# Loading 32 conditioning tiles inside the S5 loop instead of ahead of it

## The chip, the cores and the metric

One core of a Trainium2 chip runs the kernel. The metric is device time in microseconds (us), the median of several executions. PE is TensorE, DVE is VectorE, ACT is ScalarE, POOL is GpSimd, and SP is the queue from which most loads are issued.

## The reference

One decoder layer on x of 1024 tokens by 1024 channels, all in f32, cut to what matters here:

```python
cond = silu(c)                                   # one vector of 1024
mod = cond @ ada_w + ada_b                       # 6 * 1024 values
sh1, sc1, gt1, sh2, sc2, gt2 = split(mod, 6)
h = rmsnorm(x, norm_mix_w) * (1 + sc1) + sh1     # first norm
q, f, i, g, u = split(h @ w_in)
mixed = concat([hgrn2(q, f, i, g), s5(u)]) @ w_out
x = x + gt1 * mixed                              # gate 1
h2 = rmsnorm(x, norm_ffn_w) * (1 + sc2) + sh2    # second norm
x = x + gt2 * peer(h2)                           # gate 2
out = rmsnorm(x, final_norm_w)
```

The hgrn2 part is a gated linear recurrence with 4 heads, s5 is a complex diagonal recurrence with 32 groups, and peer picks 16 of 16384 experts for each token and head.

## The kernel before

The product `cond @ ada_w` is not done on PE. `ada_w` lies in 48 tiles of 128 x 1024 (512 KB each), and for each tile DVE multiplies it with the broadcast `cond` and sums along the row (line 193), which gives one column of `mod`. Tiles 0 to 15 are scale and shift of the first norm and are needed at once; they go through a ring of 10 buffers called `ada`. Tiles 16 to 47 (gate 1, second norm, gate 2) are first needed after the S5 loop, in `out_proj`, `norm_T` of the second norm and `row_consts`. They go through the ring `row`, 5 buffers that they share with the tiles of x.

Ahead of the S5 loop stand `u_proj` (the S5 inputs, matmuls of line 328, weights loaded at line 323) and the first norms (line 288). `s5_setup` is a long row of tiny DVE instructions that makes the tables of powers. For each of 8 blocks of S5 groups `s5_tables` then lets POOL build `bsrc` (lines 493 to 495) and the cosine tables (521 to 523), DVE build `ca`, and PE transpose `bsrc` (line 528) and multiply (535). `s5_scan` (lines 554 to 579) runs one block, with DVE at 558 to 575. In the same loop `head_pieces` spreads the four HGRN heads: `hgrn_in` (four projections, line 328, and DVE at 683 to 700) and `hgrn_out` (DVE at 728 to 783, PE at 743).

No engine's order is written out by hand: a scheduler takes the instructions in program order and puts each into its engine's row by a timeline of its own. Every engine then runs its row strictly in that order, and so does the SP queue. The helper `issue_after(later, earlier)` is a hint to that scheduler about order; it adds no semaphore. `marks["base"]` is the list of projection matmuls made so far, two for each weight tile.

Of the kernel before, what the change touches and what calls it, by code (L numbers as in the profile page):

```python
# [10 lines left out]
F32 = mybir.dt.float32  # L11
# [11 lines left out]
P = 128  # L23
S = 1024
D = 1024
# [38 lines left out]
NROW = 5  # L64
# [27 lines left out]
def hymba_kernel(  # L92
# [22 lines left out]
    nc = tc.nc  # L115
# [3 lines left out]
    def T(pool, shape, dt, tag, bufs=None):  # L119
        return pool.tile(shape, dt, name=f"{tag}_{next(cnt)}", tag=tag, bufs=bufs)  # L120
# [13 lines left out]
    gp = ctx.enter_context(tc.tile_pool(name="gp", bufs=1, side="right"))  # L134
# [51 lines left out]

    mod = T(cst, [P, 48], F32, "mod")

    def ada(n0, n1, pool=None):
        for n in range(n0, n1):  # L190
            at = T(pool, [P, D], F32, "ada", bufs=10) if pool else T(gp, [P, D], F32, "row", bufs=NROW)
            nc.sync.dma_start(at, ada_t[n])
            nc.vector.tensor_tensor_reduce(
                out=at, in0=at, in1=cond["B"], scale=1.0, scalar=0.0, op0=ALU.mult, op1=ALU.add,
                accum_out=mod[:, n : n + 1],
            )
        TT(mod[:, n0:n1], mod[:, n0:n1], adab[:, n0:n1], ALU.add)
# [4 lines left out]
    def load_x(c, rows=False):  # L202
        t0, nt = CHUNKS[c]
        if rows:
            xt = [T(gp, [P, D], F32, "row", bufs=NROW) for _ in range(NBC)]
        else:
            xt = [T(tp, [P, D], F32, "xh", bufs=NBC) for _ in range(NBC)]
        for i, xi in enumerate(xt):
            nc.sync.dma_start(xi, x[t0 + i * P : t0 + (i + 1) * P, :])
        return xt  # L210
# [49 lines left out]
    def issue_after(later, earlier):  # L260
        tc.add_manual_dep(
            later.ins, earlier.ins.name, mybir.DependencyInfo(mybir.DependencyClass.NoSync, mybir.DependencyReason.DATA),
            reason="issue order",
        )

    marks = {"base": [], "pre": [], "dense": []}
    phase = ["base"]

    def diags_of(xt):
        rstd = rstd_of(tp, xt)  # L270
        diags = []
        for tb in range(NBC):
            dg = T(tp, [P, P], F32, "diag", bufs=4)
            TS(dg, ident, rstd[:, tb : tb + 1], None, ALU.mult)
            diags.append(dg)
        return diags
# [562 lines left out]
    for o, i, ni, j, nj in pieces_:  # L839
        n = max(ni, nj)  # L840
# [380 lines left out]
    with tc.tile_pool(name="ap", bufs=1) as ap_:  # L1221
        for k in range(0, KD, 2):
            ada(8 + k, 10 + k, ap_)
            STT(s1c[:, k : k + 2], mod[:, 8 + k : 10 + k], 1.0, nmw[:, k : k + 2], ALU.add, ALU.mult)
            ada(k, k + 2, ap_)
            if k == 0:
                x2 = load_x(NCK - 2, True)
                d2 = diags_of(x2)
            for c, xt, dg in ((3, x3, d3), (2, x2, d2)):
                hTs[c] += norm_T(xt, s1c, mod[:, 0:8], None, dg, (k,))  # L1230

    def head_pieces(c, two=False):

        t = {}
        outs = []
        far = T(gp, [P, 2, 2, TC], F32, "acc") if c == 2 else None

        def last(h):
            outs.append(hgrn_out(hp, c == NCK - 1, h, t.pop(h), two, None if far is None else far[:, h // 2]))
            if not two:  # L1240
                raws.setdefault(c, []).append((outs[-1][:, 0], outs[-1][:, 1]))

        for h in range(0, HEADS, 1 if two else 2):
            if len(t) == 2:
                last(min(t))
                yield
            t[h] = hgrn_in(hp, h, hTs[c], hTs[c + 1] if two else None)
            yield
        for h in sorted(t):
            last(h)  # L1250
            yield
        if two:
            for i in range(2):
                raws[c + i] = [(outs[h][:, i], outs[h + 1][:, i]) for h in range(0, HEADS, 2)]
# [16 lines left out]
    def step(what, c):  # L1271

        nonlocal rp
        if what == "n":
            hTs[c] = norm_T(*pre[c][:1], s1c, mod[:, 0:8], None, pre[c][1])
            heads[c] = head_pieces(c)
        elif what == "h":
            next(heads[c])
        elif what == "g":
            mixes[c] = s5_out(c)  # L1280
        elif what == "o":
            xts[c] = load_x(c, c == NCK - 1)
            hg = [r for two in raws[c] for r in two]
            out_proj(c, hg + mixes[c], xts[c])
        elif what == "N":
            h2Ts[c] = norm_T(xts[c], s2c, mod[:, 24:32], CHUNKS[c][0])
        elif what in "rR":
            routes[c] = score(c, h2Ts[c], h2Ts[c + 1] if what == "R" else None)
            next(routes[c])
        elif what == "s":  # L1290
            next(routes[c])
        elif what == "p":
            choose(rp, c)
        elif what == "X":
            next(heads[NCK - 1], None)
            hpx.close()
        elif what == "Y":
            rpx.close()
            rp = tb_["r"] = rp2x.enter_context(tc.tile_pool(name="rp2", bufs=1, side="right"))
        elif what == "Z":  # L1300
            tbx.close()

    hgrn_consts(hp)
    with tc.tile_pool(name="sp", bufs=1) as sp:
        prm = s5_setup(sp)
        tabs = [s5_tables(sp, b, prm, "hg") for b in range(2)]
        pieces = head_pieces(0, True)
        for b in range(NGB):
            s5_scan(sp, b, tabs[b])
            if b + 2 < NGB:  # L1310
                tabs.append(s5_tables(sp, b + 2, prm, "tr"))
            if b == N2B:
                step("n", 2)
            next(pieces, None)
            if b < 4:
                ada(16 + 8 * b, 24 + 8 * b)
            if b == PRB:
                for c in (2, 3):
                    pre[c] = load_x(c, True)
                    pre[c] = pre[c], diags_of(pre[c])  # L1320
        for _ in pieces:
            pass
# [120 lines left out]
```

## Time and profile before

| | |
|---|---|
| median of 3 runs | 3045.52 us (3045.49 to 3056.46) |
| the profiled execution | 3048.81 us, its span 3047.0 us |
| PE busy in the span | 2778.7 us (91%) |
| DVE busy in the span | 2520.5 us (83%) |
| mean granted PE clock | 0.964 of full speed |

The profiled execution is 3.3 us (0.1%) above the median of the runs, and 1.8 us of it lie outside the span. A row of the profile names the line, the engine and the tiles; times are from the start of the span.

### The profile page before, as it was taken

The page shows a single profiled execution, that of the slowest core. Times are in us where ns is not written, and L with a number is a line of the kernel's source. Part 1 is how long each engine was busy: PE and PEld are TensorE (multiplying, and loading weights), DVE is VectorE, ACT ScalarE, POOL GpSimd, SP SyncE. Part 2 cuts the span into 40 slices and gives each one's busy share as a digit, 9 for nine tenths or more (in the row PEclk, how much of TensorE's full clock was granted, in tenths as well). Part 3 has the DMA queues.
Part 4 walks back from the last instruction along what each step waited for, and adds up shares of the span by engine and source line. Part 5 has one row for each costly group of instructions (what it writes and reads, how often), then busy time and mean ns, then how long its engine had stood idle before and what let it go on. Part 6 is the DMA issues. An engine that isn't in the chain of part 4 may idle for free.

```text
span 3047.0 us, 45997 instructions
## 1 busy us (share of the span) xinstructions
PE 2778.7 (91%) x16071; PEld 2492.1 (82%) x16071; DVE 2520.5 (83%) x5862; ACT 1011.4 (33%) x2089; POOL 1132.2 (37%) x1043
## 2 busy tenths in 40 slices
PE   6898989989989999999879999999999999999970
PEld 5777879878878899999878888888888888888850
DVE  7868835987799999997867888887988887888987
ACT  4223432322211755654623222222222222222210
POOL 1754100031111013333334554544545454545645
PEclk9999999999999999999989999999999999999985
DMA  9722344486754469989999998999999898999967
GB/s 335 260 76 62 103 145 143 127 272 207 247 175 139 177 234 340 322 317 345 345 324 334 338 323 309 327 323 318 309 339 349 296 318 305 321 310 336 329 242 268
DMA packets 375112, 814.06 MB, mean 267 GB/s; under 512 B 60000, under 2 KB 153824, under 8 KB 369760
## 3 DMA queue, kind: packets, MB, share of 16 engines
q0 software_dynamic: 110592, 402.70, 37.6%
q1 hardware_dynamic: 226096, 386.12, 36.7%
q10 hardware_dynamic: 38192, 22.31, 2.6%
q8 instruction: 126, 2.06, 0.3%
q14 instruction: 106, 0.87, 0.1%
HBM read 730.96 MB, written 80.05 MB: 266 GB/s over the span
## 4 chain that ended last, share of the span: by engine, by line
PE 49%; DMA 17%; DVE 16%; issue 9%; POOL 6%; ACT 3%; ACTq 0%; SPq 0%; POOLq 0%; DVEq 0%
PE mm L1081 21%; PE mm L328 12%; DMA vraw<-in_v_rows_dram 5%; DMA row<-in_v_rows_dram,ei 4%; POOL row L947 4%; PE hg L1157 4%; PE tr L1157 3%; PE s L1157 3%; DVE acc L988 2%; DVE row L972 2%; DMA row<-in_u_rows_dram,ei 1%; PE s L1045 1%; PE hg L743 1%; PE s L1046 1%; DMA S<-sd 1%
## 5 line engine op out<-in xcount | busy, mean ns | idle before, releaser
L1081 PE MATMUL mm<-h2T,w 128*128 128x320 f32 x6144 | 950.6, 314 | 45.5 <-ACT S L1083 39.8
L1081 PEld LDWEIGHTS mm<-h2T,w 128*128 128x128 f32 x6144 | 920.1, 191 | 53.8 <-ACT S L1083 44.2
L947 POOL DMA_INDIRECT row<-in_u_rows_dram,ei x384 | 458.0, 1193 | 1247.4 <-DVE dots L972 700.3
L947 POOL DMA_INDIRECT row<-in_v_rows_dram,ei x384 | 511.9, 1333 | 474.4 <-DVE acc L988 389.2
L328 PE MATMUL mm<-hT,w 128*128 128x256 f32 x2304 | 530.7, 384 | 9.2 <-DMA w<-in_w_q_dram 3.8
L988 DVE SCALAR_TENSOR_TENSOR acc<-row,dots,acc 128x1024 f32<-128x1024 f32 x381 | 488.2, 1281 | 44.4 <-DMA row<-in_v_rows_dram,ei 41.3
L328 PEld LDWEIGHTS mm<-hT,w 128*128 128x128 f32 x2304 | 433.3, 193 | 66.7 <-issue 5.0
L972 DVE CUSTOM_DVE_ANT_0 row<-row,h2n 128x1024 f32<-128x1024 f32 x384 | 463.5, 1218 | 26.6 <-DMA row<-in_u_rows_dram,ei 26.6
L1157 PE MATMUL hg<-v,W 128*128 128x512 f32 x1296 | 356.4, 396 | 31.2 <-ACT v L257 19.4
L1157 PE MATMUL s<-v,W 128*128 128x512 f32 x1296 | 351.4, 393 | 2.8 <-DVE dacc L1170 2.0
L1157 PE MATMUL tr<-v,W 128*128 128x512 f32 x1248 | 339.0, 391 | 5.2 <-ACT v L257 2.8
L257 ACT CAST v<-vraw 128x512 fp32r<-128x512 f32 x256 | 158.8, 621 | 515.0 <-DMA vraw<-in_v_rows_dram 291.2
L1157 PEld LDWEIGHTS hg<-v,W 128*128 128x128 f32 x1296 | 245.5, 191 | 87.0 <-ACT v L257 21.3
L1157 PEld LDWEIGHTS s<-v,W 128*128 128x128 f32 x1296 | 244.6, 189 | 56.1 <-DVE dacc L1170 3.0
L1157 PEld LDWEIGHTS tr<-v,W 128*128 128x128 f32 x1248 | 234.3, 189 | 56.4 <-ACT v L257 3.6
L258 DVE TENSOR_TENSOR v<-vraw,v 128x512 fp32r<-128x512 f32 x256 | 175.8, 687 | 118.1 <-ACT v L257 114.9
L257 ACT CAST w<-raw 128x512 fp32r<-128x512 f32 x256 | 158.8, 620 | 214.9 <-PE mm L1081 179.5
L258 DVE TENSOR_TENSOR w<-raw,w 128x512 fp32r<-128x512 f32 x256 | 175.6, 687 | 54.3 <-ACT w L257 47.7
L1083 ACT ACTIVATE S<-mm 128x320 f32<-128x320 f32 x256 | 109.0, 437 | 243.8 <-PE mm L1081 198.0
L257 ACT CAST W<-S 128x640 fp32r<-128x640 f32 x128 | 93.4, 731 | 218.9 <-PE s L1157 58.1
L1100 DVE TENSOR_TENSOR S<-S,gt 128x640 f32<-128x640 f32 x128 | 104.2, 821 | 41.9 <-DMA S<-sd 36.2
L1048 ACT ACTIVATE Gs<-s 128x256 f32<-128x256 f32 x320 | 97.6, 389 | 43.6 <-PE s L1046 37.4
(375 smaller groups left out, 3200.7 us busy)
## 6 DMA issues: line engine op xcount, KB each, us to landing
raw<-in_u_t_dram SPq DMA_DIRECT2D x256, 256.0 KB
vraw<-in_v_rows_dram SPq DMA_DIRECT2D x256, 256.0 KB
gd<-Gs SPq DMA_DIRECT2D x40, 1024.0 KB
gt<-gd SPq DMA_DIRECT2D x32, 1280.0 KB
w<-in_w_in_dram SPq DMA_DIRECT2D x56, 512.0 KB
w<-in_w_q_dram SPq DMA_DIRECT2D x48, 512.0 KB
sd<-S SPq DMA_DIRECT2D x60, 320.0 KB
S<-sd SPq DMA_DIRECT2D x60, 320.0 KB
```

The source lines that it names most:

```text
L257: nc.scalar.copy(hi, src)
L258: return nc.vector.tensor_tensor(lo, src, hi.bitcast(F32), ALU.subtract)
L328: ins = nc.tensor.matmul(out, w[:, k * P : (k + 1) * P], rhs[k], start=(k == 0), stop=(k == nk - 1))
L743: nc.tensor.matmul(blk(pt, c), blk(lh, c), blk(rh, c), start=True, stop=True)
L947: g = nc.gpsimd.indirect_dma_start(out=t, out_offset=None, in_=table, in_offset=bass.IndirectOffsetOnAxis(ap=idx, axis=0))
L972: nc.vector.tensor_tensor_reduce(out=ut, in0=ut, in1=h2, scale=1.0, scalar=0.0, op0=ALU.mult, op1=ALU.add, accum_out=dots[:, j : j + 1],)
L988: STT(acc, vt, w[:, j : j + 1], acc, ALU.mult, ALU.add)
L1048: nc.scalar.mul(gq[c][:, :, o8 + o4 : o8 + o4 + 4], pg[:, :, c * NI : (c + 1) * NI].rearrange("p t i -> p i t"), 1.0 / GSC,)
L1081: nc.tensor.matmul(pt, wk[:, i, kc], h2T[k][:, j, cs_], start=(n == 0), stop=(n == 3 * KD - 1))
L1083: ACT(g[:, cs_], pt, AF.Gelu)
L1100: TT(gv, gv, gtile[0][:, :, e % IG, :], ALU.mult)
L1157: nc.tensor.matmul(pv[tb], ws[e][:, a, tb * P : (tb + 1) * P], v2[:, b, :], start=(e == s and n == 0), stop=(e == s + SLAB - 1 and n == 2),)
```

## The change

The loop body that handles tiles 16 to 47 moves from iterations 0 to 3 of the S5 loop to iterations 2 to 5. The tiles get a ring of their own in the pool of the loop, `ada` with 3 buffers, in place of the 5 of `row`. Each load is told to be issued after the projection matmul that is 20 marks (five weight tiles) back from the last one made so far in the program.

```diff
-    def ada(n0, n1, pool=None):
+    def ada(n0, n1, pool=None, after=None):
         for n in range(n0, n1):
-            at = T(pool, [P, D], F32, "ada", bufs=10) if pool else T(gp, [P, D], F32, "row", bufs=NROW)
-            nc.sync.dma_start(at, ada_t[n])
+            at = T(pool, [P, D], F32, "ada", bufs=10 if after is None else 3) if pool else T(gp, [P, D], F32, "row", bufs=NROW)
+            ld = nc.sync.dma_start(at, ada_t[n])
+            if after is not None:
+                issue_after(ld, after)
...
-            if b < 4:
-                ada(16 + 8 * b, 24 + 8 * b)
+            if b >= 2 and b < 6:
+                ada(8 * b, 8 + 8 * b, sp, marks["base"][-20])
```

Line numbers above 194 are higher by 2 in the changed kernel: the multiply of line 193 is 195 there, 328 is 330, 528 is 530, 558 is 560.

The SP queue, from the last x tile of the second chunk on. Before, the conditioning tiles (`row` from `in_ada_t_dram`) stand between the weight tiles of `u_proj(0)` (`w_160` to `w_169`):

```order
L209 DMA row_360<-in_x_dram 128x1024
L192 DMA row_1344<-in_ada_t_dram 128x1024
L192 DMA row_1347<-in_ada_t_dram 128x1024
L192 DMA row_1350<-in_ada_t_dram 128x1024
L192 DMA row_1353<-in_ada_t_dram 128x1024
L323 DMA w_160_580<-in_w_in_dram 128x1024
L192 DMA row_1356<-in_ada_t_dram 128x1024
L192 DMA row_1359<-in_ada_t_dram 128x1024
L323 DMA w_163_602<-in_w_in_dram 128x1024
```

In the changed kernel the first of them stand here, between weight tiles of the second HGRN head (`w_386` to `w_400`):

```order
L325 DMA w_391_1504<-in_w_in_dram 128x1024
L192 DMA ada_1876<-in_ada_t_dram 128x1024
L192 DMA ada_1879<-in_ada_t_dram 128x1024
L192 DMA ada_1882<-in_ada_t_dram 128x1024
L325 DMA w_395_1527<-in_w_in_dram 128x1024
L192 DMA ada_1885<-in_ada_t_dram 128x1024
L192 DMA ada_1888<-in_ada_t_dram 128x1024
L192 DMA ada_1891<-in_ada_t_dram 128x1024
L192 DMA ada_1894<-in_ada_t_dram 128x1024
L192 DMA ada_1897<-in_ada_t_dram 128x1024
L325 DMA w_400_1553<-in_w_in_dram 128x1024
```

All 32 loads moved past the weights of `u_proj(0)` and of the first head, and the weight tiles of the second to fourth head now stand behind some of them.

PE, the transposes of the first S5 table (`hg_990` from `bsrc`). Before, they stand behind the second weight tile of `u_proj(0)`:

```order
L328 MATMUL mm_601<-hT_524,w_163_602 128x256 x2
L328 MATMUL mm_601<-hT_532,w_163_602 128x256 x2
L328 MATMUL mm_601<-hT_540,w_163_602 128x256 x2
L528 MATMUL hg_990<-ident_69,bsrc_936 128x128 x4
L328 MATMUL mm_623<-hT_548,w_166_624 128x256 x2
```

In the changed kernel they stand in the norm of the second chunk (`tr_515`, `tr_523`):

```order
L290 MATMUL tr_515<-diag_391,row_360 128x128
L290 MATMUL tr_523<-diag_389,row_359 128x128
L290 MATMUL tr_523<-diag_391,row_360 128x128
L530 MATMUL hg_990<-ident_69,bsrc_936 128x128
L537 MATMUL hg_998<-ca_957,bb_924 16x128 x4
L530 MATMUL hg_990<-ident_69,bsrc_936 128x128
```

They moved ahead of all of `u_proj(0)`, whose 64 matmuls and the rest of the norm now queue behind them.

DVE, the scan of the third S5 block (`z_423` before, `z_407` after). Before, it follows the second block's work and a table, ahead of the scores of the first head (`sc_678`):

```order
L513 TENSOR_TENSOR uc_385_1466<-ident_69,dd_811 16x64
L558 TENSOR_TENSOR z_423_1642<-s_421_1632,xh_1207 128x512
L559 TENSOR_TENSOR z_424_1643<-s_422_1633,xh_1207 128x512
L494 TENSOR_TENSOR uc_450_1708<-bcin_1671,ppi_815 128x144
L560 TENSOR_TENSOR z_423_1642<-z_423_1642,z_424_1643 128x512
L537 TENSOR_TENSOR kp_1485<-kp_1485,uc_385_1466 16x4x16
L744 COPY_PREDICATED sc_678<-masks_680,hg_1764 128x512
```

In the changed kernel it stands behind all scores of the first head and behind the last eight conditioning tiles, which follow each other without a gap (the last two are shown):

```order
L195 ISA ada_2805,mod_98<-ada_2805,h2n_92 128x1024
L195 ISA mod_98 128x1
L195 ISA ada_2808,mod_98<-ada_2808,h2n_92 128x1024
L195 ISA mod_98 128x1
L199 TENSOR_TENSOR mod_98<-mod_98,colt_94 128x8
L560 TENSOR_TENSOR z_407_1592<-s_405_1582,xh_1207 128x512
L561 TENSOR_TENSOR z_408_1593<-s_406_1583,xh_1207 128x512
```

The 32 multiplies moved from the stretch of `s5_setup` into that of the first two heads, and the third scan moved back behind them.

## Rows read from the trace of the kernel before

**Rows 1.** The page: engines over the span (busy, share, count), and the last chain.

```profile
PE 2778.7 (91%) x16071; PEld 2492.1 (82%) x16071; DVE 2520.5 (83%) x5862; ACT 1011.4 (33%) x2089; POOL 1132.2 (37%) x1043
PE 49%; DMA 17%; DVE 16%; issue 9%; POOL 6%; ACT 3%; ACTq 0%; SPq 0%; POOLq 0%; DVEq 0%
```

**Rows 2.** Busy time by stretch: PE, PEld, DVE, ACT, POOL; clock, DMA share, GB/s.

```profile
69.20:141.00 71.80, 59.50 (x280) 48.81 (x279) 66.94 (x155) 20.11 (x33) 50.38 (x60) 0.91 0.85 281
135.46:258.00 122.54, 113.29 (x605) 93.16 (x605) 86.85 (x166) 45.81 (x66) 73.02 (x106) 0.97 0.30 89
258.00:340.00 82.00, 73.20 (x477) 63.94 (x478) 76.79 (x180) 33.74 (x51) 32.49 (x49) 1.00 0.25 70
340.00:420.00 80.00, 68.99 (x400) 62.42 (x400) 46.15 (x118) 36.83 (x52) 0.00 (x0) 0.94 0.41 120
1060.00:1200.00 140.00, 139.91 (x1111) 137.38 (x1110) 134.43 (x436) 79.86 (x212) 31.66 (x27) 1.00 0.78 279
```

**Rows 3.** Waits of PE from 69 to 141 us: total, times, longest.

```profile
PE hg L528 <- POOL bsrc L495: 11.6, 7, 2.7
```

**Rows 4.** Line 193 over the whole span, and from 45 to 135.4 us (busy, mean ns).

```profile
L193 DVE CUSTOM_DVE_ANT_0 row<-row,h2n x32: 1204/1214/2276, 52.9 to 140.2; 128x1024 f32<-128x1024 f32 x32
L193 DVE CUSTOM_DVE_ANT_0 row<-row,h2n 128x1024 f32<-128x1024 f32 x31 | 40.0, 1294 | 0.8 <-DMA row<-in_ada_t_dram 0.8
```

**Rows 5.** Timeline of DVE, 52 to 259 us: start, duration, instruction.

```profile
52.90 1.23 DVE L193 CUSTOM_DVE_ANT_0 row<-row,h2n 128x1024 f32<-128x1024 f32 x1 [0.26 <-DMA row<-in_ada_t_dram]
...
84.00 1.22 DVE L193 CUSTOM_DVE_ANT_0 row<-row,h2n 128x1024 f32<-128x1024 f32 x1
...
85.40 0.23 DVE L436 TENSOR_SCALAR cin<-k,nsg 128x32 f32<-128x32 f32 x1
...
103.59 1.21 DVE L193 CUSTOM_DVE_ANT_0 row<-row,h2n 128x1024 f32<-128x1024 f32 x1
...
135.46 0.53 DVE L683 TENSOR_SCALAR f<-sf,oml,lb 128x512 f32<-128x512 f32 x1
...
258.34 0.67 DVE L783 TENSOR_TENSOR xx<-hg,rstd 128x512 f32<-128x512 f32 x1
```

**Rows 6.** Timeline of POOL, first S5 table, and its first cosine instruction.

```profile
85.71 1.43 POOL L494 TENSOR_TENSOR us<-bcin,cin 128x64 f32<-128x64 f32 x1 [5.37 <-DVE cin L436]
...
98.76 0.41 POOL L494 TENSOR_TENSOR us<-bbs,rpi 128x128 f32<-128x128 f32 x1
99.25 1.31 POOL L495 TENSOR_TENSOR bsrc<-us,us 128x128 f32<-128x128 f32 x1
...
106.52 1.10 POOL L521 TENSOR_TENSOR acc<-fine,coarse 128x512 f32<-128x512 f32 x1 [4.33 <-DVE coarse L475]
```

**Rows 7.** Timeline of PE: the second norm, and `u_proj(0)` up to the first head.

```profile
69.20 1.05 PE L288 MATMUL tr<-diag,row 128*128 128x128 f32 x8
...
116.77 1.05 PE L535 MATMUL hg<-ca,bb 128*16 128x128 f32 x8
117.75 12.35 PE L328 MATMUL mm<-hT,w 128*128 128x256 f32 x56
```

**Rows 8.** Timeline of ACT: the first sigmoid of the first head.

```profile
132.87 1.28 ACT L678 ACT_TABLE_LOAD   x1 [14.39 <-DVE uc L494]
134.16 0.60 ACT L678 ACTIVATE sf<-mm 128x512 f32<-128x512 f32 x1
```

**Rows 9.** DVE from 135.46 to 340 us by line, seven scans and tables.

```profile
L564 DVE TENSOR_TENSOR_SCAN xr<-z,z 128x512 f32<-128x512 f32 x7 | 8.7, 1247 | 0.1
L495 DVE TENSOR_TENSOR ca<-uc,uc 128x144 f32<-128x144 f32 x24 | 8.3, 347 | 0.4 <-PE s L579 0.2
L575 DVE TENSOR_TENSOR xhs<-xr,z 128x512 f32<-128x512 f32 x7 | 6.8, 977 | 0.1
L560 DVE TENSOR_TENSOR z<-z,z 128x512 f32<-128x512 f32 x7 | 4.9, 700 | 0.1
```

**Rows 10.** The chain up to 460 us: loads of conditioning tiles (start, us).

```profile
45.35 7.42 DMA row<-in_ada_t_dram
54.17 3.97 DMA row<-in_ada_t_dram
```

## The prediction, made before the changed kernel had run

> **What bounds the kernel now.** I read the page first: PE is busy for 91% of the span and DVE for 83%, and the chain that ended last is half PE [rows 1]. A gain must therefore come out of PE's idle time in the stretches that the change touches, 45 to about 340 us; everything behind them runs in a fixed order on each engine and starts as much earlier or later as they end. Second, the busy times by stretch. From 69 to 141 us DVE is nearly full (66.9 of 71.8 us), PE is not (59.5) and its clock is granted at 0.91 [rows 2]. Third, PE's waits there: 11.6 us, all for POOL's `bsrc`, seven times [rows 3]. PE never waits for a weight tile there, so the loads as such, though they keep the DMA engines 0.85 busy, hold up nothing on PE. What holds it up is the row DVE, POOL, PE: the tables. Fourth, from 135 to 258 us PE is busy for 113.3 of 122.5 us and DVE for 86.9, and from 258 to 340 us DVE for 76.8 of 82 (0.94) [rows 2]. So DVE has idle time just where the tiles go, but not beyond it.
>
> **What is removed ahead of the loop.** 31 of the 32 multiplies of line 193 leave the stretch from 45 to 135 us, where they took 40.0 us of DVE [rows 4].
> - *DVE's setup.* Thirteen of them, the first at 52.90 and the last at 84.00 us, stand ahead of `cin`, for which POOL waits until 85.7 [rows 5, 6]. At 1.21 us [rows 4], with the 0.8 us that DVE waited for their loads, they are 16.5 us: `cin` comes at about 69.2.
> - *POOL's first table.* From 85.71 to the end of the fourth part of `bsrc` at 100.56 are 14.85 us for 17 instructions; those that meet a line 193 take some 1.4 us, the others 0.41 [rows 6]. Without the multiplies I count 17 x 0.43 = 7.3 us: the four parts of `bsrc` come at about 72.6, 73.8, 75.1 and 76.5.
> - *PE's first table.* Its transposes now stand inside the norm that PE begins at 69.2 us [rows 7], so it waits there from about 69.8 to 72.6, and some 1 us more for the other parts: 4 us.
> - *PE's second table.* In the new order POOL builds it behind a cosine instruction that needs the `coarse` table. That instruction ran at 106.52 us [rows 6], with 23 multiplies ahead of it on DVE, the last of them at 103.59 [rows 5]: 106.5 - 23 x 1.21 = 78.7. Two cosine instructions (1.10 us) and six others (0.43) make the table's first `bsrc` ready at 83.5. PE is there at about 80: 4 us. In sum 8 us of waits, against 11.6 before, and the norm and `u_proj(0)` now stand behind them.
> - *PE up to the first head.* Before, the head's first projection (32 of the 56 matmuls, 7.0 us) ends at 124.8 [rows 7], but its sigmoid starts at 134.16, since ACT stood 14.39 us behind a load that waited for DVE [rows 8]. After, PE has from 69.2 us on 7 us of norm, five projections of 7.0 and 3 us of tables, 45 us, and 8 of waits: 122.3. ACT's row has no such load ahead of the sigmoid any more, so with 1.28 and 0.60 us for ACT, line 683 runs on DVE at about 124.7 instead of 135.46 [rows 5]. **This term is a gain of 10.8 us.** Its bounds: a gain of 3, if the waits for the tables double, and of 19, if they vanish.
>
> **What is added in the loop.** All 32 multiplies and their loads. I follow DVE from line 683 to line 783 of the first head, at 258.3 us before [rows 5]. DVE's busy time of 86.85 us between them [rows 2] grows by 31 x 1.23 = 38.1 us (1.21 and the read-out). The order also puts one more scan and one more table ahead of line 783: a scan is one of 1.25 us, one of 0.98 and six of 0.69, 6.4 us, and a table twelve of 0.34, 4 us [rows 9]: 10.4 us, which are then saved behind it. In sum 135.4 us of DVE work from 124.7 on, so to 260 us at the earliest: **DVE becomes the bound of this stretch.** How densely it can work is the open value. The lowest is 0.71, as it worked there before (86.85 of 122.5) [rows 2]; that would be some 190 us and a loss of over 40, but those gaps are what the multiplies, which depend on nothing but their loads, can fill. The highest is 1. I take 0.95, between the 0.94 of 258 to 340 us and the 0.96 that DVE reaches from 1060 to 1200 us (134.4 of 140) [rows 2]: 142.5 us, to 267.2. With the work done ahead (10.4 / 0.95 = 10.9) taken off, that is 256.3 against 258.3 before. **This term is a loss of 8.8 us.** Each 0.05 of density is 7 to 8 us; 1 makes a gain of 8.6 in all, 0.90 a loss of 5.2.
>
> **The loads.** They are hidden so long as a tile lands before DVE comes to it. A ring of three lets a load go when the tile three ahead has been multiplied, so tiles in a row come at (landing + 1.21) / 3. Landings of 3.97 and 7.42 us stand in the trace [rows 10], the latter while the DMA engines were 0.85 busy; in the loop they are 0.30 busy [rows 2], so I take 4: 1.73 us a tile. Most tiles have other DVE work between them and are hidden; the last eight follow each other and take 13.8 instead of 9.8 us. These 4 us are part of the density. SP is moved past too: weight tiles of heads two to four stand behind tiles that wait for DVE. By the times above each lands 10 us or more before PE needs it, so I cost this at nothing; it is the first cover to go if DVE falls behind.
>
> **Sum.** -10.8 + 8.8 = -2.0 us. Behind 340 us DVE has idle time again (46 of 80) [rows 2], and the few reorderings of later rows I count as nothing. The profiled execution would be 3046.8, and, as it lies 3.3 us above the median of the runs, I predict **3043.5 us**.
>
> **A rule weighed.** An instruction of DVE that meets POOL's work was slow in places: line 193 has a median of 1.21 us and a longest of 2.28 [rows 4]. Yet from 45 to 135 us, where POOL was busy for most of the time, its mean was 1.294: 0.08 us each, 2.6 us for all 32. The Trainium skill, in "SBUF — State Buffer", section "Who interferes with whom", says that a DVE instruction with two SBUF inputs and a GpSimd instruction that reads SBUF exclude each other for the whole instruction. By that rule the move would cost DVE up to a whole POOL instruction for each meeting, and it speaks against the change; by the trace's mean the cost is the 2.6 us, which DVE paid before too.
>
> **Rivals.**
> - *PE sets the pace in the loop.* The multiplies fall into DVE's 35.7 idle us of the stretch, as the order has them between other work. Then the 10.8 us stay, and of PE's 18 idle us from 135 to 340 (9.2 and 8.8) [rows 2] half or all go too: 3026 to 3017. For it: PE was the fuller engine there. Against: DVE's sum leaves only 0.05 of slack.
> - *The ring of three paces DVE*, the case on the slow side. Place: the second to fourth group of eight, in and behind the scores of the first head. If a load lands in 6 us (between 3.97 and 7.42), tiles come every 2.4 us: 9.5 us more for the last eight and, where half of the sixteen ahead are not covered, as much again. DVE stands still, and behind it the scans and the weight tiles on SP: 3053 to 3063. It decides from landings of about 5 us on.
> - *DVE and POOL exclude each other in the loop.* If six in ten of the 32 (POOL's busy share there, 73 of 122.5 us [rows 2]) meet a POOL instruction and lose 0.9 us, near the 1.06 between median and longest, that is 17 us more: 3060. The mean of 1.294 us speaks against it. The rule named above would bring this about.
>
> **How the numbers follow.** My case holds at 0.56, from 3035 (a start at its upper bound) to 3052 (density 0.90 and a start 3 us worse). PE's pace has 0.21, the ring 0.18, the excluding engines 0.05. The range reaches into the outer cases until some 0.2 is left out: 3020 to 3062. A measurement of this kernel tells 0.5%, 15 us, from no change. PE's pace is mostly beyond that (0.18), and my case with the best start adds 0.02: faster 0.20. The ring and the excluding engines are beyond it with 0.14. Same has 0.66.
>
> **What would show it.** In the changed profile line 195 no longer stands between 45 and 125 us; POOL's first `bsrc` ends at 72 to 74; PE waits for `bsrc` at 70 and at 80 us, 8 us in sum; line 685 (683 before) first runs near 125. From there to line 785 (783 before), near 267, DVE is 0.95 busy and PE has idle time behind its hoisted projections. At 340 us both kernels are at the same place within 8 us. I am wrong if DVE's density is below 0.88 or if PE, not DVE, waits least in that stretch; if line 195 waits for its loads by more than 8 us in sum; or if the waits at 70 to 90 us are twice mine.

## The result, and the profile after

The changed kernel takes 3071.03 us (median; 3063.24 to 3085.13), the kernel before, run beside it, 3048.02 us (3043.24 to 3056.46). The ratio is 1.007, 95% interval 1.0051 to 1.0088: **slower by 0.7%, some 21 us**, above the upper end of the predicted range. The profiled execution has a span of 3068.0 us against 3047.0.

To see where the 21 us arise I follow one instruction that both kernels run in the same place: the first copy with the gate in `out_proj(0)`, behind the S5 loop (line 802, 804 after). From the timelines of ACT, before and after (start, duration, instruction):

```profile
414.96 0.84 ACT L802 ACTIVATE tmp<-mm,mod 128x256 f32<-128x256 f32 x2 [0.17 <-PE mm L328]
```
```profile
437.43 0.84 ACT L804 ACTIVATE tmp<-mm,mod 128x256 f32<-128x256 f32 x2 [1.03 <-PE mm L330]
```

The changed kernel is 22.5 us behind there, and still 21.0 behind at the last row that is written out, 3038.8 us before. So the loss is complete when the S5 loop ends. This **position** is what I compare below. It is read from one execution of each kernel, and no kernel was profiled twice, so how well it repeats is not known. Kernels that share their first part (the kernel before with e3_before_y_ub and e5_one_late, the changed kernel with e2b_ring2) start the first head 0.3 to 1.0 us apart, so I read nothing into differences of 1 or 2 us. In the dense stages far behind the loop the difference between two kernels wanders by 10 us and more. The expectations call the position "424 us"; its place before is 414.96, and each lead or lag below is the difference to that.

The start came much as foretold. From the changed kernel's timelines of DVE, POOL and PE, and PE's waits from 69 to 141 us (total, times, longest):

```profile
126.53 0.55 DVE L685 TENSOR_SCALAR f<-sf,oml,lb 128x512 f32<-128x512 f32 x1 [15.34 <-ACT sf L680]
```
```profile
72.24 0.45 POOL L497 TENSOR_TENSOR bsrc<-us,us 128x128 f32<-128x128 f32 x1
```
```profile
PE tr L290 <- ACT hT L293: 3.9, 3, 3.2
PE hg L530 <- POOL bsrc L497: 2.8, 1, 2.8
```

The first head starts at 126.53 instead of 135.46 [rows 5], and PE waits 2.8 us for `bsrc` instead of 11.6 [rows 3]. Behind it all is lost, and more. The busy times by stretch (PE, PEld, DVE, ACT, POOL; clock, DMA share, GB/s), to be read beside [rows 2]:

```profile
69.20:141.00 71.80, 65.14 (x330) 55.74 (x330) 30.29 (x78) 26.86 (x42) 36.64 (x67) 0.95 0.44 125
126.50:292.00 165.50, 132.75 (x667) 108.63 (x666) 124.39 (x237) 44.55 (x63) 63.47 (x75) 0.91 0.49 164
258.00:340.00 82.00, 63.79 (x371) 52.01 (x372) 74.43 (x167) 28.43 (x44) 55.02 (x78) 0.90 0.19 52
340.00:420.00 80.00, 74.54 (x470) 67.70 (x469) 59.25 (x147) 40.91 (x58) 0.97 (x4) 0.98 0.43 120
```

From line 685 to line 785 of the first head (291.99 us) DVE is busy for 124.39 of 165.5 us. That is 0.75, not the 0.95 that I took, so DVE is not what bounds this stretch. POOL is not either: from 198 to 258 us it hardly works, and from 258 to 340 it catches up. What everyone waits for stands at 249 us. First ACT's copies of the S5 result, with the first copy of the kernel before ahead of them, then PE, DVE and POOL around them, from their timelines (the bracket is the idle time before, and what ended it):

```profile
168.97 0.59 ACT L581 COPY h2n<-s 128x512 f32<-128x512 f32 x1 [0.26 <-PE s L579]
```
```profile
248.94 0.58 ACT L583 COPY h2n<-s 128x512 f32<-128x512 f32 x1 [12.76 <-DVE mod L195]
251.62 0.58 ACT L583 COPY h2n<-s 128x512 f32<-128x512 f32 x1 [2.09 <-DMA ys<-h2n]
265.51 0.59 ACT L583 COPY h2n<-s 128x512 f32<-128x512 f32 x1 [10.10 <-PE s L581]
```
```profile
249.58 2.08 PE L556 MATMUL s<-ubt,tb 128*128 128x128 f32 x8 [6.17 <-ACT h2n L583]
```
```profile
232.92 1.22 DVE L195 CUSTOM_DVE_ANT_0 ada<-ada,h2n 128x1024 f32<-128x1024 f32 x1 [4.61 <-DMA ada<-in_ada_t_dram]
...
247.67 1.23 DVE L195 CUSTOM_DVE_ANT_0 ada<-ada,h2n 128x1024 f32<-128x1024 f32 x1 [0.39 <-DMA ada<-in_ada_t_dram]
248.82 0.08 DVE L195 DVE_READ_ACCUMULATOR2_ANT mod<- 128x1 f32 x1
...
251.69 0.69 DVE L560 TENSOR_TENSOR z<-s,xh 128x512 f32<-128x512 f32 x1 [2.58 <-PE s L556]
...
256.73 1.22 DVE L566 TENSOR_TENSOR_SCAN xr<-z,z 128x512 f32<-128x512 f32 x1
```
```profile
202.40 0.45 POOL L497 TENSOR_TENSOR bsrc<-us,us 128x128 f32<-128x128 f32 x1
261.55 1.77 POOL L525 TENSOR_TENSOR xh<-acc 128x512 f32<-128x512 f32 x1 [58.69 <-DVE xr L576]
```

The last conditioning multiply and its read-out end at 248.9 us, and in that moment the first copy of an S5 result starts, 12.76 us after ACT was free for it. Both copies at 249 and 251.6 are of scans whose matmuls were done some 70 and more us before. The reason is one line that I had not read against the change: `condB`, the conditioning vector that every multiply of line 195 reads, and `yg`, into which `s5_scan` copies its result, are tiles of the same tag `h2n` in a pool with one buffer for each tag. The result of scan 1 can be written only when the last reader of the conditioning vector is done. Until then the results of scans 1 and 2 hold both PSUM buffers of tag `s5`, so scan 3 can't start (6.17 us of PE's own waiting; the rest PE fills with projections), POOL can't build the next table, and six scans and their tables stand in a row behind 249 us. Before, the last multiply was at 140.2 us [rows 4] and the first copy at 168.97, so the two never met.

### The profile page after: what moved, and what is told of

Read it like the earlier page. It is cut to its first block, busy times and chain, and to the rows that moved or that the text cites. A ratio compares the mean times of both kernels' runs of the same rounds, so it can differ in the third digit from the quotient of the medians.

```text
span 3068.0 us, 45993 instructions
## 1 busy us (share of the span) xinstructions
PE 2784.0 (91%) x16071; PEld 2492.6 (81%) x16071; DVE 2507.4 (82%) x5862; ACT 1003.9 (33%) x2086; POOL 1113.3 (36%) x1043
## 4 chain that ended last, share of the span: by engine, by line
PE 46%; DMA 15%; issue 14%; DVE 13%; POOL 9%; ACT 2%; SPq 0%; ACTq 0%; POOLq 0%; DVEq 0%
PE mm L1083 18%; PE mm L330 13%; POOL row L949 8%; DMA row<-in_v_rows_dram,ei 5%; DMA vraw<-in_v_rows_dram 4%; PE hg L1159 3%; PE s L1159 3%; PE tr L1159 3%; DVE row L974 2%; DMA row<-in_u_rows_dram,ei 1%; DVE acc L990 1%; PE hg L745 1%; DMA ada<-in_ada_t_dram 1%; PE s L1047 1%; PE s L1048 1%
```

## The experiments

All were compared with the kernel before, on the same chip. The theories: **A**, the hold on the one buffer `h2n`; **B**, DVE has too much work between the first head's sigmoid and its output (the term of my forecast); **C**, the loads and the ring of three pace DVE. The results, with the start of the first head on DVE (line 683, 685 or 686) and that of the first S5 copy on ACT, which tells whether the hold is there:

| kernel | first head, us | first S5 copy, us | position: lag (+) or lead (-), us | time / time before (95%) |
|---|---|---|---|---|
| before | 135.46 | 168.97 | 0 | 1 |
| changed | 126.53 | 248.94 | +22.5 | 1.007 (1.0051 to 1.0088) |
| e1_y_in_ub | 126.49 | 146.90 | +4.1 | 1.0006 (0.9985 to 1.0027) |
| e3_before_y_ub | 135.11 | 168.52 | -6.8 | 0.9979 (0.996 to 0.9998) |
| e5_one_late | 134.59 | 226.69 | +5.9 | 1.0015 (0.9992 to 1.0038) |
| e7_quarter | 126.22 | 231.93 | +7.8 | 1.001 (0.9988 to 1.0033) |
| e10_quarter_y_ub | 125.94 | 146.57 | -8.1 | 0.9988 (0.9967 to 1.001) |
| e2_y_ub_ring2 | 124.56 | 145.04 | +2.0 | 1.0033 (1.0008 to 1.0059) |
| e2b_ring2 | 127.49 | 256.19 | +30.9 | 1.0084 (1.0052 to 1.0116) |
| e11_cond_own | 123.85 | 144.60 | +2.8 | 1.0014 (0.9992 to 1.0036) |
| e6_spread | 124.39 | 144.85 | +1.6 | 1.0029 (1.0007 to 1.0052) |
| e8_behind | 126.88 | 147.51 | +14.0 (behind the multiplies) | 1.0102 (1.0072 to 1.0132) |
| e12_half | 124.18 | 145.25 | -3.5 | 1.0006 (0.9981 to 1.003) |
| e12c_24 | 129.00 | 151.05 | -0.1 | 1.001 (0.9988 to 1.0032) |

**The hold alone.** The result goes into the block's own input tile, which is dead by then and has two buffers:

```diff
-        yg = T(gp, [P, GB, NC], F32, "h2n")
+        yg = ub
```

> The changed kernel, but each block's S5 result is written over the block's own input tile ub (two buffers) instead of the single buffer h2n that also holds the conditioning vector. Theory A (the result of scan 1 cannot leave PSUM until the last conditioning multiply has read h2n, so scans 3 to 8 wait): the copy of the first S5 result, which first ran at 248.9 us, runs before 170; PE's wait for h2n (6.2 us) and POOL's idle time for xr (59 us) are gone; the 23 us lost against the kernel before come back, 3035 to 3050. Theory B (DVE has too much work between the first head's sigmoid and its output): DVE's work is the same, 3060 to 3075. Theory C (the ring of three and the landings pace DVE): the waits for ada of 13.6 us stay, 3060 to 3075.

```profile
146.90 0.59 ACT L583 COPY ubt<-s 128x512 f32<-128x512 f32 x1 [3.98 <-PE s L581]
```

The first copy runs at 146.90, behind the matmuls of its own scan (line 581), the wait for `h2n` is gone, and 18.4 of the 22.5 us come back, with the same multiplies on DVE. The time, 3052.7 us, lies between what A (up to 3050) and what B and C (from 3060) had foretold. The waits for `ada` fall from 12.7 to 3.8 us as well (120 to 420 us). POOL's waits for `xr` are 59.1 us in three (after: 89.5), so that part of A's expectation was only half right. DVE's line 195 in the two kernels, 120 to 300 us, the changed kernel first:

```profile
L195 DVE CUSTOM_DVE_ANT_0 ada<-ada,h2n x32: 1201/1225/2289, 141.1 to 247.7; 128x1024 f32<-128x1024 f32 x32
...
  ACT h2n L583: 12.8, 1
```
```profile
L195 DVE CUSTOM_DVE_ANT_0 ada<-ada,h2n x32: 1195/1220/2292, 141.0 to 261.4; 128x1024 f32<-128x1024 f32 x32
```

The last multiply is later here (261.4), and yet the loop ends earlier: nobody waits for it any more.

**The control.** The same line on the kernel before.

> The kernel before with the same edit of the S5 result's tile alone, as a control. There the last conditioning multiply is at 140 us and the first copy of an S5 result at 169, so the shared buffer held up nothing. A, B and C: no difference beyond 4 us from the kernel before (3044 to 3052). If it is faster by 10 us or more, what the first run gains says nothing on the change.

6.8 us ahead, and a ratio just below 1: more than I expected, though less than the 10 that would have spoiled the first run. The copies did not wait for the buffer there; the fourth scan and a table stand in another order. The edit is thus not neutral: against this control, which differs from e1 by the move of the tiles alone, e1 is 10.9 us behind and not 4.1. How much of the 18.4 us is the hold itself needs another kernel (e11, below).

**One late reader.** 31 tiles stay; only the last is read late:

```diff
             if b < 4:
-                ada(16 + 8 * b, 24 + 8 * b)
+                ada(16 + 8 * b, 24 + 8 * b - (b == 3))
+            if b == 5:
+                ada(47, 48, sp, marks["base"][-20])
```

> The kernel before with only the last of the 32 tiles moved late (fifth turn of the loop, ring of three, issued by the same mark); 31 stay where they were. It adds no work to DVE and no load worth naming, but the conditioning vector is read once more behind the second head's q, at about 241 us in the kernel before, and the third scan (206.7 us there) then stands behind it. A: the first S5 result is copied only after that multiply, at 220 to 245 us, the third scan comes some 40 us late, and the time is 3053 to 3068. B and C: within 4 us of the kernel before, 3044 to 3052.

From the timelines of DVE and ACT of that kernel:

```profile
225.43 1.23 DVE L195 CUSTOM_DVE_ANT_0 ada<-ada,h2n 128x1024 f32<-128x1024 f32 x1 [3.62 <-DMA ada<-in_ada_t_dram]
...
237.83 1.22 DVE L566 TENSOR_TENSOR_SCAN xr<-z,z 128x512 f32<-128x512 f32 x1
```
```profile
226.69 0.59 ACT L583 COPY h2n<-s 128x512 f32<-128x512 f32 x1 [5.61 <-DVE mod L195]
```

A single multiply of 1.23 us, with no other work moved, holds the first copy back from 168.97 to 226.69 and the third scan from 206.65 to 237.83, and costs 5.9 us of position. The mechanism is A's; the time, 1.0015, stands at the border of what the theories expected and does not tell it from no change.

**Less work, the hold kept.** A quarter of the columns for the late tiles:

```diff
+            w = D if after is None else D // 4
             nc.vector.tensor_tensor_reduce(
-                out=at, in0=at, in1=cond["B"], scale=1.0, scalar=0.0, op0=ALU.mult, op1=ALU.add,
+                out=at[:, :w], in0=at[:, :w], in1=cond["B"][:, :w], scale=1.0, scalar=0.0, op0=ALU.mult, op1=ALU.add,
```

> The changed kernel with the 32 late multiplies over 256 of their 1024 columns (the other three quarters of those sums are left out), loads and places kept. A multiply falls from 1.21 to about 0.4 us, so some 26 us of DVE's work go, while the last one still has to read h2n before the first S5 result is copied. A: the last multiply comes at 215 to 235 us instead of 249, so the wait shrinks by part only: 3055 to 3068. B: the loss goes with the work, 3033 to 3048. C: tiles still come by their landings, 3058 to 3072.

14.6 of the 22.5 us come back; the time, 3053 us, lies between what A and B expected. The rows of the late multiplies (120 to 420 us) show how:

```profile
L196 DVE CUSTOM_DVE_ANT_0 ada<-ada,h2n x32: 401/426/1491, 140.8 to 231.5; 128x256 f32<-128x256 f32 x32
...
  DMA ada<-in_ada_t_dram: 25.0, 17
```

The multiplies are done 16.2 us sooner (231.5 instead of 247.7), and with them the hold ends 17.0 us sooner: less work and a shorter hold are one edit here. To part them, the same with the hold away:

> Both edits in one: the S5 result in ub, and the 32 late multiplies over a quarter of their columns (the rest of those sums is left out). In the first four runs either edit alone took back most of the 22.5 us by which the changed kernel is behind at 424 us: 4.1 behind with the result in ub, 7.8 with a quarter of the columns; and the result in ub made the kernel before 6.8 earlier there. If the hold on h2n (A) and DVE's work (B) are the whole loss, no loss is left and the early start of the first head (8.3 us) shows: 10 to 17 us ahead of the kernel before at 424 us, 3031 to 3040. If what stays behind with the result in ub is the pace of the loads and the ring (C), it stays: within 5 us of the kernel before at 424 us, 3045 to 3053.

8.1 us ahead at the position, against 4.1 behind with whole multiplies: **with the hold away, three quarters of DVE's multiply work are worth 12.2 us**. Against e7 (7.8 behind), the hold with a quarter of the columns is worth 15.9. The lead is just under the foretold 10 to 17, but the time (3046.7, ratio 0.9988) lies in C's range and not in the 3031 to 3040 us of A and B. The waits for loads stay, 11.6 us, and against the control e10 loses 7.9 us between the first head and the position (9.2 ahead there, 1.3 here), so a part for the loads and their places is not ruled out.

**The ring.** With the hold away, and then with it:

```diff
-            at = T(pool, [P, D], F32, "ada", bufs=10 if after is None else 3) if pool else T(gp, [P, D], F32, "row", bufs=NROW)
+            at = T(pool, [P, D], F32, "ada", bufs=10 if after is None else 2) if pool else T(gp, [P, D], F32, "row", bufs=NROW)
```

> The changed kernel with the S5 result in ub and a ring of two instead of three for the 32 tiles. C: a tile comes every (landing + 1.21) / 2 instead of / 3; with the waits for ada of 4.7 us in the run with a ring of three, they become 15 to 30 us, and the time grows by 8 to 15 us, to 3058 to 3068. A and B: the waits fall into DVE's other idle time, no more than 4 us against the ring of three: 3048 to 3057.

> The changed kernel with a ring of two instead of three, the S5 result still in h2n: the partner of the next run, and a second look at the ring with the hold in place. A: the last multiply comes some us later than at 249 us, since the tiles come slower, and the scans with it: 20 to 32 us behind the kernel before at 424 us, 3068 to 3080. C: half as many tiles on their way make the loss half as large again, over 34 us behind at 424 us, 3082 or more.

Without the hold a ring of two waits 8.6 us for its tiles instead of 3.8, and the loop ends 2.1 us earlier than with three; 1.9 of these stand at the first head already. Its time came out longer (3057.6 us, at the border of the two expectations; 1.0033 against 1.0006, intervals that overlap), behind the loop, and I don't read a cause into that. With the hold the waits are 25.3 us, the first copy runs 7.3 us later than in the changed kernel, and the position is 8.5 us worse. So a smaller ring shows a cost at the position only where the hold is there, as A has it.

**The conditioning vector in a buffer of its own,** the S5 result still in `h2n`; for want of space with a ring of two:

```diff
+        own = T(sp, [P, D], F32, "cond", bufs=1)
+        nc.scalar.copy(own, cond["B"])
+        cond["B"] = own
         prm = s5_setup(sp)
```

> The changed kernel with a ring of two and the conditioning vector copied once, ahead of the loop, into a buffer of its own, which the late multiplies read; the S5 result stays in the single buffer h2n. It takes away the hold and nothing else, where the run with the result in ub also gave the result two buffers in place of one (worth 6.8 us on the kernel before). A: the first S5 result is copied before 180 us; if the whole difference of 18 us between the changed kernel and its twin with the result in ub was the hold, it is 0 to 6 us behind the kernel before at 424 us, as the twin with a ring of two was (2.0), 3046 to 3055; if 6.8 of the 18 belonged to the second buffer, 7 to 12 behind, 3054 to 3061. If the hold is not the cause: 20 or more behind, 3068 or more.

```profile
144.60 0.59 ACT L583 COPY h2n<-s 128x512 f32<-128x512 f32 x1 [4.13 <-PE s L581]
```

2.8 us behind, where its twin with the hold (e2b) is 30.9 behind and its twin with the result in `ub` 2.0. Of the 28.2 us between e2b and e11, 3.6 stand at the first head already. The second buffer for the result makes 0.8 us at the position here (1.5 counted from the first head), too little to tell from none: the difference is the hold. Both times, 3077.1 us of e2b and 3053.6 of e11, lie where A had them. The 6.8 us that the same edit gave the kernel before do not come with it here; where they come from is open.

**Other places for the tiles,** each with the result in `ub`: four tiles behind each of the eight turns; all behind the loop, in the next stage's pool; half or a quarter of them late.

```diff
-            if b >= 2 and b < 6:
-                ada(8 * b, 8 + 8 * b, sp, marks["base"][-20])
+            ada(16 + 4 * b, 20 + 4 * b, sp, marks["base"][-20])
```

> The changed kernel with the S5 result in ub and the 32 tiles in groups of four, one behind each of the eight turns of the loop, instead of eight behind turns two to five. B: the same work on DVE in the same stretch, spread; the scans are delayed by less at a time, 1 to 6 us better than in groups of eight: 3045 to 3052. C: the waits for ada vanish and with them 3 to 5 us. If the bunches of eight hold up the scans, 8 us or more better: 3038 to 3045.

2.5 us better in position than in groups of eight, but 2.1 of these stand at the first head already, so a gain from spreading is not shown; the time, 3055.5 us (1.0029), is no better and above what was foretold.

```diff
-    STT(s2c, mod[:, 32:40], 1.0, nfw, ALU.add, ALU.mult)
-    row_consts()
     tb_["p"] = tbx.enter_context(tc.tile_pool(name="tb", bufs=2))
...
     nc.sync.dma_start(keyst, keys)
+    ada(16, 48, tb_["p"], marks["base"][-20])
+    STT(s2c, mod[:, 32:40], 1.0, nfw, ALU.add, ALU.mult)
+    row_consts()
```

> The 32 tiles leave the start as in the change, the S5 result is in ub, but the multiplies stand behind the S5 loop, with the tiles in a ring of ten in the next stage's pool. There DVE was busy for 25 of 80 us (420 to 500), where 40 us of multiplies cost nothing. A and B: nothing in the loop holds up the scans and DVE is as free as before; the start of the first head 8 us earlier and the 6.8 us of the result in ub both last, 10 to 17 us ahead at 424 us: 3031 to 3040, which would beat both kernels. C in another form: the 32 loads of 0.5 MB now meet the weight tiles from 340 us on, PE waits for weights there, 3045 to 3060.

Neither expectation named what came, and it is the slowest kernel of all; its position is taken at ACT's fourth copy of line 862 (524.99 us; 511.00 before, line 860), since the gate's copy itself now waits for the multiplies. Up to 340 us it went as A and B said: at 339 us it is 10.7 us ahead of the kernel before in the copies of the S5 results and 18 in the rows of ACT beside them. Then the multiplies fell between the links of a head's output norm. The timelines of DVE and PE, and the same norm in the kernel before:

```profile
390.62 0.68 DVE L782 TENSOR_REDUCE ms<-z 128x4 f32<-128x512 f32 x1
...
394.25 0.17 DVE L237 TENSOR_SCALAR rstd<-rstd 128x4 int32<-128x4 int32 x1
394.32 1.22 DVE L195 CUSTOM_DVE_ANT_0 ada<-ada,h2n 128x1024 f32<-128x1024 f32 x1
...
396.31 1.22 DVE L195 CUSTOM_DVE_ANT_0 ada<-ada,h2n 128x1024 f32<-128x1024 f32 x1 [0.68 <-DMA ada<-in_ada_t_dram]
...
403.46 0.69 DVE L785 TENSOR_TENSOR xx<-hg,rstd 128x512 f32<-128x512 f32 x1
```
```profile
404.21 1.11 PE L788 MATMUL tr<-ident,xx 128*128 128x128 f32 x4 [15.13 <-DVE xx L785]
```

```profile
401.13 0.69 DVE L780 TENSOR_REDUCE ms<-z 128x4 f32<-128x512 f32 x1 [6.22 <-ACT z L778]
...
404.51 0.69 DVE L783 TENSOR_TENSOR xx<-hg,rstd 128x512 f32<-128x512 f32 x1
```
```profile
405.26 1.11 PE L786 MATMUL tr<-ident,xx 128*128 128x128 f32 x4 [9.72 <-DVE xx L783]
```

A link of the norm takes 0.17 us. With seven multiplies of 1.22 us between the links, four of them with a wait for their load, DVE needs 12.8 us from the reduction to line 785, where the kernel before needs 3.4. Of a lead of 10.5 us at the reduction 1.1 are left. PE stands still for 15.13 us here, but for 9.72 in the kernel before as well. The rest of the swing, from 1 us ahead to 14 behind, comes later; the first copy with the gate, which needs the last multiplies, runs at 438.07 instead of 414.96. How that rest divides I did not part.

```diff
             if b < 2:
                 ada(16 + 8 * b, 24 + 8 * b)
             elif b < 4:
                 ada(16 + 8 * b, 24 + 8 * b, sp, marks["base"][-20])
```

> Half of the change: the S5 result in ub, the first 16 of the 32 tiles where they stood before (ahead of the loop's first projections, ring of five rows), the other 16 behind turns three and four in a ring of three. The 2 x 2 of hold and work put DVE's work in the loop at 12 us for three quarters of 32 multiplies; 16 cost about 8. DVE has half of the 40 us less to do before the first head, so that head starts 4 to 8 us earlier. With the 6.8 us of the result in ub: 3 to 8 us ahead of the kernel before at 424 us, 3039 to 3048, no different from the kernel before with the result in ub alone (6.8 ahead). If few multiplies fit into idle time of DVE: 10 to 16 ahead, 3030 to 3038.

> As the half, but with 24 tiles where they stood and only 8 late, in turn four. Eight multiplies in the loop cost some 3 us by the same price, or nothing if they fall into idle time; the first head starts 2 to 5 us earlier. 6 to 11 us ahead of the kernel before at 424 us, 3036 to 3045.

The half is 3.5 us ahead, in the expected 3 to 8; the quarter 0.1 ahead, where 6 to 11 were expected; both times (3050.9 and 3049.6 us) came out at no change and above the foretold ranges. So a smaller part of the move does not show a gain either: in position each of these kernels is behind the control (6.8 ahead), in which no tile is moved. That control is the one version whose time came out below the kernel before by more than its interval, by 0.2% (0.02 to 0.4%); as one of thirteen comparisons, and so close to the edge, it may be chance.

## Why the prediction was wrong

**The start** was right: -10.8 us foretold, -8.9 measured at line 685 (126.53 against 135.46). The first `bsrc` ends at 72.7 (72.6 foretold), the waits for `bsrc` are 2.8 us instead of 8, and 3.9 us for ACT's `hT` take part of their place.

**The step that failed** is the sentence on density: "those gaps are what the multiplies, which depend on nothing but their loads, can fill". It asked what the multiplies wait for, and not who waits for them. They are the last readers of the one buffer `h2n`, whose next owner is the first S5 result. The order showed the third scan behind all multiplies, and I counted the scans' work and not why they stood there. The forecast has no term for this wait; in its place the runs show the first S5 result held until 248.94 us, DVE at a density of 0.75 instead of 0.95, and a loss of 18.4 us that goes when the hold goes. The kernels with the hold:

| kernel with the hold | first S5 copy, us | position, us |
|---|---|---|
| e5_one_late | 226.69 | +5.9 |
| e7_quarter | 231.93 | +7.8 |
| changed | 248.94 | +22.5 |
| e2b_ring2 | 256.19 | +30.9 |

The first 57.7 us of delay cost little (e5, which moves one multiply only: 5.9). From 248.94 to 256.19, between two kernels that differ by the ring alone, the position grows by 8.5 us for 7.3, so there the price is about one for one; from 231.93 to 248.94 it grows by 14.6 for 17.0, but e7 has less work on DVE as well. Of the kernels with the result in `ub` and whole multiplies in the loop none is more than 4.1 behind. Taking the hold away by either of two edits gives 18.4 us with a ring of three and 28.2 with a ring of two (30.9 - 2.8, e11). That the hold is the cause of most of the loss is thus shown.

**The term of DVE's work** was too small as well. The forecast of -2.0 us at the end of this stretch is in truth one of e1, which is at +4.1. There the first head starts 9.0 us earlier than before, so 13.1 us are lost behind it, where 8.8 were foretold; of the 6.1 us between forecast and e1 the start makes 1.8 and this term 4.3. Against the control, whose order profits from the same edit, the loss behind the first head is 19.5 us. Three quarters of the columns make some 12 us of it; what the loads, their places and the last quarter make was not parted. In e1 the whole time, 1.0006, is the "no change" that I forecast, but its interval does not tell -2 us from +4, and my density was too high all the same; busy time of e1 from line 685 to line 785 (276.57 us), columns as above:

```profile
126.50:276.00 149.50, 126.48 (x670) 105.52 (x669) 126.52 (x240) 44.44 (x63) 71.24 (x83) 0.92 0.56 182
```

126.5 us in 149.5 are 0.85, below the 0.88 that I had named as the point where I would be wrong.

**The rivals.** PE did not set the pace; its clock and its busy time both fell. The ring of three: its waits for loads are 12.7 us, above the 8 that I had named, and the landings 4.5 us in the median (4 assumed), but it doesn't carry the loss, since a ring of two without the hold ends the loop no later. Its numbers (3053 to 3063) were nearest to the measured time for another reason. DVE and POOL excluding each other is there, but small. The multiplies in the loop, in the changed kernel and in e1 (count, busy us, mean ns, idle time before):

```profile
L195 DVE CUSTOM_DVE_ANT_0 ada<-ada,h2n 128x1024 f32<-128x1024 f32 x32 | 42.4, 1331 | 12.8 <-DMA ada<-in_ada_t_dram 12.7
```
```profile
L195 DVE CUSTOM_DVE_ANT_0 ada<-ada,h2n 128x1024 f32<-128x1024 f32 x32 | 44.4, 1395 | 3.8 <-DMA ada<-in_ada_t_dram 3.8
```

Before, the mean was 1294 ns [rows 4]. In the changed kernel the 22 multiplies that no instruction of POOL overlaps take at most 1.23 us each; of the ten that one overlaps seven take 1.33 to 2.29 (counted from the timelines). The Trainium skill's rule ("SBUF — State Buffer", section "Who interferes with whom") has those longer that meet POOL, and the trace agrees in kind. Beyond 1.22 us each, the meetings cost 3.5 us in the changed kernel, where POOL stands idle beside half of the multiplies because of the hold, and 5.7 in e1, against 2.4 before: 1 to 3 us more, and not the 17 of the rival. My sum, at 1.23 us each with the read-out, had nothing for it.

**What stays open:** why the control gains 6.8 us. It may be the order that the edit brings with it, but no run isolates it. Against the control, the tiles' move with neither hold nor most of the work (e10) is worth 1.3 us, too little to tell from none; the start's 9.2 us then are not seen in full, and which chain takes them was not tested.

## What to carry to other kernels

Before moving a reader later, look up every buffer that it reads, and in its pool the tag and number of buffers: the next tile with that tag can't be written until the moved reader is done, and in a list of the moved instructions this shows only as other work standing behind them for no reason of its own. An instruction that is moved into "idle time" of an in-order engine must also be priced at the places where that idle time lies: between the short links of a chain on which another engine waits, each lengthens the chain by its own time (3.4 us became 12.8 in e8). And a position inside the program, one instruction that all versions run, shows differences of a few us where whole times tell only 6 to 10; profile one kernel twice to learn how well it repeats, which was not done here.

## What the runs showed of the hardware

PE's granted clock fell where PE was left without work. Busy time by stretch of the changed kernel and of e1, columns as above:

```profile
236.00:258.00 22.00, 11.32 (x48) 9.56 (x48) 11.50 (x18) 2.22 (x5) 0.00 (x0) 0.76 0.51 183
```
```profile
236.00:258.00 22.00, 21.22 (x125) 17.33 (x124) 21.96 (x50) 8.18 (x14) 8.46 (x6) 1.00 0.69 232
```

The mean of 0.76 lies between the two levels, 1.2 and 2.4 GHz; with the hold away it is 1.00 in the same stretch, PE being busy for 21.22 of 22 us. In e2b, where PE is busy for 4.97 us of it, the mean is 0.71. From 258 to 340 us the clock is 0.90 in the changed kernel and 0.85 in e1, both with PE busy for 64 to 66 us, against 1.00 before at 73.2 [rows 2]. A wait on PE may thus be paid a second time in the matmuls behind it; I had put no term for that, and how much of the 22.5 us it makes was not measured. One place shows the price: the eight matmuls with which the third scan begins take 2.08 us behind the hold (249.58 us, above) and 1.05 us in the kernel before, where the clock is 1.00 from 198 to 258 us:

```profile
197.07 1.05 PE L554 MATMUL s<-ubt,tb 128*128 128x128 f32 x8
```
